# Folding a modulation row into expert rows, and re-ordering three starts, in a two-layer trunk kernel on Trainium2

## The chip, the cores and the metric

The kernel runs on one core of one Trainium2 chip. The metric is device microseconds (us) of one execution, and the time of a version is the median of its runs. The core has TensorE (PE) for matrix products, VectorE (DVE), ScalarE (ACT) and GpSimd (POOL) for the rest, and SyncE (SP), which here only issues transfers. PE's clock has two levels, 1.2 and 2.4 GHz; a granted clock of 0.50 in a row is the lower one and 1.00 the higher.

## The reference

Two layers run over 256 latent tokens and 256 context tokens of 1024 numbers. Each has a mixer part and an expert part, and each part ends in a residual sum whose second term is multiplied by a row of the modulation (`g1`, `g2`; `cg1`, `cg2` for context tokens). Layer 1 is the last one, and its context tokens are not computed beyond the keys.

```python
def rmsnorm(x, g):
    xf = x.astype(jnp.float32)
    y = xf * lax.rsqrt(jnp.mean(xf * xf, axis=-1, keepdims=True) + EPS)
    return (y * g.astype(jnp.float32)).astype(x.dtype)
...
    for e in range(N_EXPERTS):
        a = jax.nn.silu(t @ w_gate[e]) * (t @ w_up[e])
        y = y + gate[:, e:e + 1] * (a @ w_down[e])
...
        h = modulate(rmsnorm(x_lat, norm1_g[l]), sh1, sc1)
...
        x_lat = x_lat + g1 * hybrid_mixer(p, u, v, q_a, g, keys, lp, rope_tabs)
        h2 = modulate(rmsnorm(x_lat, norm2_g[l]), sh2, sc2)
        x_lat = x_lat + g2 * moe(h2, router_w, router_b, w_e_gate[l], w_e_up[l], w_e_down[l])
        if not last:
...
            x_ctx = x_ctx + cg2 * moe(hc2, router_w, router_b, w_e_gate[l], w_e_up[l], w_e_down[l])
```

`gate` is zero but for a token's two chosen experts, so only chosen pairs of token and expert are computed.

## The kernel before

Tokens lie in tiles of 128 partitions: t = 0 and 1 are latent, t = 2 and 3 context. Products that need full precision are done as three matmuls on high and low halves (`mm3`, L201 to L203): ACT casts the high half (L209 for weights), and `low` (L195) subtracts it to get the low half. `low` counts its calls in `spl[0]` and gives every fourth to GpSimd, the others to VectorE (`L198` is the subtraction of both). The order on each engine is the order of the code as a scheduler releases it, with `issue_after`, `behind` and `keep_in_program_order` as hand-set edges.

**Start (to 50 us).** The modulation is a product of the condition vector with a large weight that arrives in pieces. Each piece is four matmuls (L254); after the fourth of a group, ACT evicts the sum (L259), PE transposes it (L265) and DVE reduces it. `x_half(0)` and `x_half(1)` make the two halves of the normed, modulated input `xh` and `xl`; the second half needs the second group of pieces. `win_k` (L433) multiplies `xh` and `xl` with the weights of the columns `kr` and `kv0`.

**First dispatch (498 to 540 us).** After the router, `pick` (L1125) finds each token's two experts in a chain of small DVE operations, beside which `warm(5)` keeps PE busy with products that nobody reads. `first_idx` (L1152) ranks the tokens. Experts' work is cut into *jobs*: 128/g places of one expert, each row cut into g parts that lie in different partitions (g is 2 or 4). Job 0's tokens are picked by matmuls with a one-hot matrix (`dispatch`, L1171), which reads the rows in SBUF. Job 1's tokens are listed (`first_list`, L1189) and gathered from DRAM by GpSimd (`gather`, L1301). Then GpSimd scatters the lists of all places to DRAM in eight instructions (L1247), and gathers the tokens of jobs 2 and 3. Each job's rows are transposed on PE (L1419), copied by ACT (L1560) and multiplied with the gate and up weights (L1655); a SiLU on ACT (L1681), a product on DVE and a transposition (L1631) follow.

**Down (`down`, L1577).** The down product of a job (L1586) lies in PSUM as `py`. In layer 0 ACT scales it by the token's weight into `y2` (L1595), casts it to the high half and DVE makes the low half (L1603 to L1608), and PE adds both to the accumulators `acc` of the latent tokens with a one-hot matrix (L1620). `y2` is also scattered to DRAM for the context tokens. In layer 1 DVE does the scaling and multiplies with the modulation row `g2x` in one instruction (L1593). There are 25 downs in layer 0.

**Layer boundary (811 to 854 us).** `keep` (L1711) multiplies each quarter of `acc` with the row `g2b` (L1714), adds it to the residual `xres` (L1715) and takes its sum of squares on ACT (L1716). Two weights are split ahead (L1796), one low half on DVE and one on GpSimd. A loop for overflowing places (L1727) is tested and, in the profiled execution, not entered. `x_pair` (L364) takes the root from the sums, transposes and scales both latent tiles and makes `xh` and `xl`, on which PE starts the input products of layer 1. `comb` (L1802) reads the context tokens' expert rows back from DRAM as `yk`, adds the two of a token and multiplies them with a row on GpSimd (L1808, L1809), and adds them to `xres` on DVE (L1810). `x_tr` (L343) norms and transposes the two context tiles, and the `kr` product (L201 at 853.77 us) is the first that needs them.

Of the kernel before, what the change touches and what calls it, by code (L numbers as in the profile page):

```python
# [105 lines left out]
def trunk(ctx: ExitStack, tc: tile.TileContext, a, out):  # L106
# [195 lines left out]
    for l in range(DEPTH):  # L302
# [118 lines left out]
        if l == 0:  # L421
# [32 lines left out]
            win_k("kr", range(2, 4))  # L454
            win_k("kv0", range(4))
# [869 lines left out]
        pends = []  # L1325
# [182 lines left out]
        acc = [[atp() for _ in range(2)] for _ in range(2)]  # L1508
# [32 lines left out]
        if last:  # L1541
            place()
            for q_ in order_[7:9]:
                early[q_] = wexp(*q_, parts=4)
# [32 lines left out]
        def down(j, aT, wd):  # L1577
# [385 lines left out]
```

## Time and profile before

| quantity | value |
|---|---|
| median of 3 runs | 1314.17 us (1310.4 to 1314.49) |
| profiled execution | 1316.32 us, span 1314.7 us, mean granted clock 0.978 |
| PE busy | 1222.2 us, 93% of the span |
| DVE, ACT, POOL busy | 610.3, 406.9, 273.3 us |
| PE waits over 0.3 us, 480 to 840 us | 23.1 us in 17 waits; the longest 4.75, 3.99 and 3.40 |

The span runs from the first to the last recorded instruction. PE is busy nearly all the time, so a change shows in the whole time where it removes a wait of PE, moves work off PE, or lifts its clock. The rows of the trace give the wait ahead of an instruction in brackets, with the engine and the line that ended it.

### The profile page before, as it was taken

The page shows a single profiled execution, that of the slowest core. Times are in us where ns is not written, and L with a number is a line of the kernel's source. Part 1 is how long each engine was busy: PE and PEld are TensorE (multiplying, and loading weights), DVE is VectorE, ACT ScalarE, POOL GpSimd, SP SyncE. Part 2 cuts the span into 40 slices and gives each one's busy share as a digit, 9 for nine tenths or more (in the row PEclk, how much of TensorE's full clock was granted, in tenths as well). Part 3 has the DMA queues.
Part 4 walks back from the last instruction along what each step waited for, and adds up shares of the span by engine and source line. Part 5 has one row for each costly group of instructions (what it writes and reads, how often), then busy time and mean ns, then how long its engine had stood idle before and what let it go on. Part 6 is the DMA issues. An engine that isn't in the chain of part 4 may idle for free. (4 is left out here: it accounts for less than half of the span.)

```text
span 1314.7 us, 23115 instructions
## 1 busy us (share of the span) xinstructions
PE 1222.2 (93%) x9372; PEld 826.7 (63%) x9372; DVE 610.3 (46%) x1374; ACT 406.9 (31%) x765; POOL 273.3 (21%) x300
## 2 busy tenths in 40 slices
PE   5899989999999998899999998799999999888986
PEld 2587656666777775555555554678988965455544
DVE  4436554546332465332222324837666854534232
ACT  4433334333222221132122223544565421111112
POOL 0324350001201012221122111535610212100000
PEclk8899999999999998999999999899999999999999
DMA  8622465657655949498999835634444589999996
GB/s 343 200 60 73 145 226 213 222 193 235 209 180 191 314 156 354 178 412 333 397 402 423 332 140 209 229 121 134 127 157 142 189 331 356 423 424 421 423 425 251
DMA packets 70639, 338.30 MB, mean 257 GB/s; under 512 B 9472, under 2 KB 21168, under 8 KB 57984
## 3 DMA queue, kind: packets, MB, share of 16 engines
q1 hardware_dynamic: 59328, 320.93, 65.2%
q0 software_dynamic: 4832, 8.09, 1.8%
q10 hardware_dynamic: 6368, 7.76, 1.7%
q8 instruction: 75, 1.23, 0.4%
q14 instruction: 36, 0.29, 0.1%
HBM read 332.37 MB, written 10.02 MB: 260 GB/s over the span
## 5 line engine op out<-in xcount | busy, mean ns | idle before, releaser
L1655 PE MATMUL mmp<-wx,wh 128*64 128x256 f32 (+1 forms) x3456 | 254.8, 329 | 9.9 <-ACT wh L1560 6.1
L1655 PEld LDWEIGHTS mmp<-wx,wh 128*64 128x64 f32 (+1 forms) x3456 | 161.5, 124 | 94.4 <-issue 34.9
L201 PE MATMUL mmp<-xh,wh 128*128 128x512 f32 (+2 forms) x576 | 210.6, 367 | 6.8 <-ACT xh L430 6.1
L203 PE MATMUL mmp<-xh,wl 128*128 128x512 f32 (+2 forms) x576 | 201.4, 350 | 0.0
L1586 PE MATMUL trp<-wx,r 128*32 128x256 f32 (+1 forms) x944 | 130.1, 480 | 7.3 <-DVE r L1633 7.3
L201 PEld LDWEIGHTS mmp<-xh,wh 128*128 128x128 f32 (+1 forms) x576 | 109.9, 192 | 31.5 <-ACT xh L430 6.6
L203 PEld LDWEIGHTS mmp<-xh,wl 128*128 128x128 f32 (+1 forms) x576 | 110.4, 192 | 18.4 <-issue 2.9
L202 PE MATMUL mmp<-xres,wh 128*128 128x512 f32 (+1 forms) x288 | 115.5, 402 | 0.0
L209 ACT CAST wh<-raw 128x1024 fp32r<-128x1024 f32 (+2 forms) x53 | 54.0, 1024 | 127.6 <-PE mmp L202 51.6
L202 PE MATMUL mmp<-xl,wh 128*128 128x256 f32 (+2 forms) x288 | 86.8, 301 | 5.2 <-DVE xl L391 5.1
L1586 PEld LDWEIGHTS trp<-wx,r 128*32 128x32 f32 (+1 forms) x944 | 44.6, 122 | 73.2 <-issue 52.1
L198 DVE TENSOR_TENSOR wl<-raw,wh 128x1024 fp32r<-128x1024 f32 (+2 forms) x44 | 52.6, 1197 | 80.9 <-ACT wh L209 80.6
L1604 DVE TENSOR_TENSOR wl<-r,wl 64x512 fp32r<-64x512 f32 x54 | 37.1, 686 | 97.6 <-ACT wl L1603 85.7
L209 ACT CAST wh<-wx 128x1024 fp32r<-128x1024 f32 (+2 forms) x55 | 55.9, 1025 | 56.7 <-issue 24.1
L1425 POOL DMA_INDIRECT ysd<-r,ixh x25 | 25.5, 1022 | 192.8 <-ACT r L1595 192.2
L1595 ACT ACTIVATE r<-trp,sel 128x512 f32<-128x512 f32 (+1 forms) x25 | 15.5, 619 | 161.7 <-PE trp L1586 160.1
L202 PEld LDWEIGHTS mmp<-xres,wh 128*128 128x128 f32 (+1 forms) x288 | 54.6, 190 | 16.0 <-DVE xres L431 2.3
L1682 DVE TENSOR_TENSOR r<-r,mmp 128x256 f32<-128x256 f32 (+1 forms) x43 | 15.9, 370 | 103.5 <-ACT r L1681 103.5
L202 PEld LDWEIGHTS mmp<-xl,wh 128*128 128x128 f32 (+1 forms) x288 | 56.1, 195 | 11.3 <-DVE xl L391 5.8
L1620 PE MATMUL atp<-wl 128*128 128x512 f32 (+1 forms) x176 | 48.8, 416 | 12.3 <-ACT wl L1607 7.3
L198 DVE TENSOR_TENSOR wl<-wx,wh 128x1024 fp32r<-128x1024 f32 (+1 forms) x44 | 55.9, 1280 | 7.3 <-ACT wh L209 7.1
L1302 POOL DMA_INDIRECT wh<-h2d,ixh x24 | 27.6, 1149 | 127.7 <-PE trp L1419 94.8
(390 smaller groups left out, 2045.6 us busy)
## 6 DMA issues: line engine op xcount, KB each, us to landing
wx<-in_wexp_dram SPq DMA_DIRECT2D x79, 2048.0 KB
raw<-in_wmod_dram SPq DMA_DIRECT2D x80, 512.0 KB
wx<-in_wexp_dram SPq DMA_DIRECT2D x44, 512.0 KB
raw<-in_win_dram SPq DMA_DIRECT2D x35, 512.0 KB
wx<-in_win_dram SPq DMA_DIRECT2D x35, 512.0 KB
raws<-in_wmod_dram SPq DMA_DIRECT2D x8, 1024.0 KB
xres<-in_wexp_dram SPq DMA_DIRECT2D x5, 1024.0 KB
trk<-in_wexp_dram SPq DMA_DIRECT2D x5, 1024.0 KB
```

Source lines behind the costliest of these rows:

```text
L198: e.tensor_tensor(dst, full, hi.bitcast(F32), op=OP.subtract)
L201: T.matmul(o, lh, rh, start=first, stop=False, skip_group_check=True)
L202: T.matmul(o, lh, rl, start=False, stop=False, skip_group_check=True)
L203: T.matmul(o, ll, rh, start=False, stop=last_, skip_group_check=True)
L209: S.copy(h[:, :n], src)
L1302: return G.indirect_dma_start(out=xg[:, :D // g], out_offset=None, in_=h2d.rearrange("r (h d) -> (r h) d", h=g), in_offset=bass.IndirectOf ...
L1425: s_i = G.indirect_dma_start(out=ysd.rearrange("r (h d) -> (r h) d", h=g), in_=y, in_offset=None, out_offset=bass.IndirectOffsetOnAxis(ap= ...
L1586: T.matmul(py[i * P // g:(i + 1) * P // g, :w], aT[:, (c % m) * P + c // m * (P // g):(c % m) * P + (c // m + 1) * (P // g)], wcols(wd, o, ...
L1604: V.tensor_tensor(hb[1][rs, cs], y2[rs, :w], yh_.bitcast(F32), op=OP.subtract)
L1620: T.matmul(acc[t][h], one[h][rs, t * P:(t + 1) * P], hb[n][rs, h * 512:(h + 1) * 512], start=(j == 1 and n == 0 and not last), stop=(n == ...
L1655: parts(g, lambda h, gs_: mms.append(T.matmul(px[gs_, i * f:(i + 1) * f], ex[:, (k % n) * P + k // n * q:(k % n) * P + (k // n + 1) * q], ...
L1682: misc["a0"] = V.tensor_tensor(a0[:, :f], a0[:, :f], px[:, f:2 * f], op=OP.mult)
```

## The change

It has seven parts.

1. *Pieces first.* At the start, `kr`'s second half of products is put behind the first piece of the second modulation group, and `kv0`'s behind the second.
2. *Early accumulators.* `warm(5)` becomes `warm(1)` and four products of the identity with `xres`, which open `acc` with the residual in it.
3. *Both first places in SBUF.* Job 1's tokens are picked by `dispatch` too; `first_list(1)` and its gather go.
4. *Row folded.* In layer 0, `y2` is made as in layer 1, by DVE with the row `g2x`; ACT makes a second copy without the row, `yc`, for the scatter. Twelve small transfers bring `g2x`, and the transfer of `g2b` goes.
5. *Shorter `keep`.* It copies `acc` to `xres` on DVE, and ACT squares straight from `acc`. Both low halves ahead are on DVE, the second behind the sum of squares. The root is begun before the pools of the expert part close.
6. *Combine later.* The first addition of `yk` waits for `x_pair`'s last `xl`.
7. *No early low halves on GpSimd.* `spl[0]` is set to -8 in `x_pair`, so the next 15 calls of `low` go to DVE.

```diff
 def x_pair():
+            rs = misc["rs"]
+            spl[0] = -8
...
-            win_k("kr", range(2, 4))
-            win_k("kv0", range(4))
+            with tc.issue_after(misc["mod", 1, 0].ins):
+                win_k("kr", range(2, 4))
+            with tc.issue_after(misc["mod", 1, 1].ins):
+                win_k("kv0", range(4))
...
-            dispatch(0, one_hot(0, r2([P, NT, P // fixed[0][2]])), False)
+            hots = [one_hot(n, r2([P, NT, P // fixed[n][2]])) for n in range(2)]
...
-            first_list(1)
-            gather(xgb[1], fixed[1][2], ix01[:, 1:2])
+            for n in range(2):
+                dispatch(n, hots[n], False)
...
-                warm(5)
+                warm(5 if last else 1)
+                for t_ in range(2):
+                    for h in range(2):
+                        acc[t_][h] = atp()
+                        if not last:
+                            tc.keep_in_program_order(T.matmul(acc[t_][h], ident, xres[:, t_, h * 512:(h + 1) * 512],
+                                                              start=True, stop=False, skip_group_check=True))
...
-            if last:
-                V.scalar_tensor_tensor(y2[:, :w], py[:, :w], sel[:, k, 2:3], g2x[g, b], op0=OP.mult, op1=OP.mult)
-            else:
-                S.activation(y2[:, :w], py[:, :w], AF.Copy, scale=sel[:, k, 2:3])
+            V.scalar_tensor_tensor(y2[:, :w], py[:, :w], sel[:, k, 2:3], g2x[g, b], op0=OP.mult, op1=OP.mult)
...
+            if not last:
+                yc = r2([P, 512])
+                S.activation(yc[:, :w], py[:, :w], AF.Copy, scale=sel[:, k, 2:3])
+                scatter(yc[:, :w], g, ixh[:, k, 1:2])
             halves(evict)
-            if not last:
-                scatter(y2[:, :w], g, ixh[:, k, 1:2])
...
-            tm = r2([P, 512])
-            V.tensor_tensor(tm, v, g2b[:, hs], op=OP.mult)
-            V.tensor_tensor(xres[:, t, hs], xres[:, t, hs], tm, op=OP.add)
-            S.activation(tm, xres[:, t, hs], AF.Square, accum_out=misc["ss"][:, t, hf:hf + 1])
+            S.activation(tm, x_ if more else v, AF.Square, accum_out=misc["ss"][:, t, hf:hf + 1])
...
-            G.tensor_tensor(yk[:, 1], yk[:, 1], yk[:, 0], op=OP.add)
+            behind(G.tensor_tensor(yk[:, 1], yk[:, 1], yk[:, 0], op=OP.add), misc["xl", 1])
```

At the start, PE's second group of pieces before (L254 is a piece, L265 the transposes of the finished group, L201 to L203 the products):

```order
L203 MATMUL mmp<-xh,wl 128x512
L201 MATMUL mmp<-xh,wh 128x512
L254 MATMUL atp<-raws,trk 32x512 x4
L202 MATMUL mmp<-xres,wh 128x512
L203 MATMUL mmp<-xh,wl 128x512
L254 MATMUL atp<-raws,trk 32x512 x4
L265 MATMUL trp<-st_69,r_286 128x128 x4
```

And after, from the second and third piece on:

```order
L254 MATMUL atp<-raws,trk 32x512 x8
L201 MATMUL mmp<-xh,wh 32x512
L202 MATMUL mmp<-xres,wh 32x512
L203 MATMUL mmp<-xh,wl 32x512
L201 MATMUL mmp<-xh,wh 32x512
L202 MATMUL mmp<-xres,wh 32x512
L203 MATMUL mmp<-xh,wl 32x512
L254 MATMUL atp<-raws,trk 32x512 x4
L201 MATMUL mmp<-xh,wh 128x512
L202 MATMUL mmp<-xres,wh 128x512
L203 MATMUL mmp<-xh,wl 128x512
L201 MATMUL mmp<-xh,wh 128x512
```

Before, all 24 products of `kr` and `kv0` stand ahead of the group's last piece. After, 12 do; 4 more stand between that piece and the transposes, and 8 behind the transposes.

At the first dispatch, PE before (L1177 is the pick of job 0, L1198 the lists, L1419 the transposes of a job's rows):

```order
L1177 MATMUL trp<-xh,r_4154 64x512 x8
L1198 MATMUL trp<-cst,r_4168 128x1 x4
L1198 MATMUL trp<-cst,r_4274 128x1 x4
L1198 MATMUL trp<-cst,r_4282 128x1 x4
L1419 MATMUL trp<-st_69,wh 128x128 x4
L1655 MATMUL mmp<-wx_3689,wh 64x256 x16
L1655 MATMUL mmp<-wx_3691,wh 64x256 x8
L1419 MATMUL trp<-st_69,wh 128x128 x2
L1655 MATMUL mmp<-wx_3691,wh 64x256 x8
L1655 MATMUL mmp<-wx_3689,wh 32x128 x32
```

And after:

```order
L1176 MATMUL trp<-xh,r_4158 64x512 x8
L1176 MATMUL trp<-xh,r_4160 32x256 x16
L1197 MATMUL trp<-cst,r_4282 128x1 x4
L1197 MATMUL trp<-cst,r_4290 128x1 x4
L1424 MATMUL trp<-st_69,wh 128x128 x6
L1655 MATMUL mmp<-wx_3689,wh 64x256 x16
L1655 MATMUL mmp<-wx_3691,wh 64x256 x16
L1655 MATMUL mmp<-wx_3689,wh 32x128 x32
```

The two transposes of job 1 have moved from within job 0's products (64x256) to before them, and 16 picking products stand where one list did.

At the layer boundary, VectorE before, from the sum of squares on (L391 are the four `xl` of `x_pair`, L1810 the context tiles' sums):

```order
L366 TENSOR_TENSOR ss<-r_ssx 128x2
L160 TENSOR_SCALAR rs<-ss 128x2
L372 TENSOR_SCALAR r_7008<-st_69,rs 128x128 x2
L386 TENSOR_SCALAR r_7016<-trp,gsc,modcol_86 128x256
L386 TENSOR_SCALAR r_7026<-trp,gsc,modcol_86 128x256
L391 TENSOR_TENSOR xl<-r_7016,xh 128x2x256
L198 TENSOR_TENSOR wl<-wx_6993,wh 128x1024
```

And after (L1806 is the second low half ahead, L1820 the context tiles' sums):

```order
L1798 TENSOR_TENSOR ss<-r_ssx 128x2
L1806 TENSOR_TENSOR wl<-wx_6671,wh 128x1024
L160 TENSOR_SCALAR rs<-ss 128x2
L369 TENSOR_SCALAR r_7072<-st_69,rs 128x128 x2
L383 TENSOR_SCALAR r_7080<-trp,gsc,modcol_86 128x256
L198 TENSOR_TENSOR wl<-wx_7062,wh 128x1024
L388 TENSOR_TENSOR xl<-r_7080,xh 128x2x256
```

A low half of 1024 columns now stands between the sum of squares and the root, and another ahead of the first `xl`. Behind the last `xl`, the context sums have taken this order (L613 reads products of PE):

```order
L198 TENSOR_TENSOR wl<-wx_7062,wh 128x1024
L198 TENSOR_TENSOR qal<-r_7171,qah 128x256
L613 TENSOR_SCALAR r_7202<-mmp,trk 128x256
L1820 TENSOR_TENSOR xres<-xres,yk 128x1024
L198 TENSOR_TENSOR qal<-r_7202,qah 128x256
L613 TENSOR_SCALAR r_7238<-mmp,trk 128x256
L1820 TENSOR_TENSOR xres<-xres,yk 128x1024
```

The second context sum has two more operations between it and the first, where one L160 stood before.

## Rows read from the trace of the kernel before

**Rows 1.** Windows by stage: PE, PEld, DVE, ACT, POOL busy; clock, DMA share, GB/s.
```profile
570.00:640.00 70.00, 70.00 (x633) 39.00 (x633) 17.74 (x40) 17.74 (x34) 13.27 (x12) 1.00 0.91 368
854.00:1000.00 146.00, 143.33 (x1023) 124.91 (x1021) 86.40 (x179) 74.61 (x138) 57.31 (x70) 0.98 0.43 134
1090.00:1308.00 218.00, 192.78 (x2256) 112.50 (x2252) 87.66 (x214) 33.37 (x72) 17.05 (x17) 1.00 0.97 400
```

**Rows 2.** Timeline, PE, at the start: start, length, instruction, [idle before].
```profile
36.08 0.39 PE L203 MATMUL mmp<-xh,wl 128*128 128x512 f32 x1
36.31 0.39 PE L201 MATMUL mmp<-xh,wh 128*128 128x512 f32 x1
...
38.28 1.06 PE L254 MATMUL atp<-raws,trk 128*32 128x512 f32 x8
40.05 0.65 PE L265 MATMUL trp<-st,r 128*128 128x128 f32 x4 [0.71 <-ACT r L259]
44.09 1.06 PE L201 MATMUL mmp<-xh,wh 128*32 128x512 f32 x2 [3.38 <-ACT xh L430]
```

**Rows 3.** Windows at the start.
```profile
42.60:49.40 6.80, 5.31 (x13) 2.99 (x14) 4.54 (x9) 3.98 (x8) 1.94 (x6) 0.50 1.02 392
49.40:60.00 10.60, 10.60 (x49) 8.07 (x47) 7.33 (x9) 6.16 (x9) 7.57 (x15) 1.00 0.61 170
```

**Rows 4.** Timeline, PE, at the first dispatch.
```profile
516.63 7.09 PE L1655 MATMUL mmp<-wx,wh 128*64 128x256 f32 x48 [0.67 <-ACT wh L1560]
523.65 0.44 PE L1419 MATMUL trp<-st,wh 128*128 128x128 f32 x2
...
530.72 3.77 PE L1655 MATMUL mmp<-wx,wh 128*32 128x128 f32 x66 [4.75 <-ACT wh L1560]
...
534.79 1.07 PE L1655 MATMUL mmp<-wx,wh 128*32 128x128 f32 x30
```

**Rows 5.** Timeline, ACT, at the first dispatch.
```profile
530.29 0.37 ACT L1560 COPY wh<-trp 128x256 f32<-128x256 f32 x1 [13.71 <-remote]
```

**Rows 6.** Timeline, POOL, at the first dispatch.
```profile
515.89 1.03 POOL L1247 DMA_INDIRECT lst<-tokid,r_ai  x1 [0.30 <-DVE r_ix L1200]
...
526.14 1.04 POOL L1302 DMA_INDIRECT xg<-h2d,r_ix  x1 [0.30 <-issue]
```

**Rows 7.** Line L1593 (layer 1): length in ns (min, median, max), first and last.
```profile
L1593 DVE SCALAR_TENSOR_TENSOR r<-trp,sel,wh x10: 750/751/752, 1109.4 to 1276.1; 128x512 f32<-128x512 f32 x10
```

**Rows 8.** Timeline, DVE, at the layer boundary.
```profile
814.70 2.60 DVE L1715 TENSOR_TENSOR xres<-xres,r 128x512 f32<-128x512 f32 x2
...
817.83 1.21 DVE L1796 TENSOR_TENSOR wl<-wx,wh 128x1024 fp32r<-128x1024 f32 x1
818.96 0.68 DVE L1715 TENSOR_TENSOR xres<-xres,r 128x512 f32<-128x512 f32 x1
...
825.67 0.69 DVE L391 TENSOR_TENSOR xl<-r,xh 128x512 fp32r<-128x512 f32 x1
826.49 3.20 DVE L198 TENSOR_TENSOR wl<-wx,wh 128x1024 fp32r<-128x1024 f32 x1
829.62 2.83 DVE L391 TENSOR_TENSOR xl<-r,xh 128x512 fp32r<-128x512 f32 x1
...
833.58 4.42 DVE L391 TENSOR_TENSOR xl<-r,xh 128x512 fp32r<-128x512 f32 x2 [0.23 <-ACT xh L390]
...
842.14 1.22 DVE L1810 TENSOR_TENSOR xres<-xres,yk 128x1024 f32<-128x1024 f32 x1
```

**Rows 9.** Timeline, POOL, at the layer boundary.
```profile
826.01 2.60 POOL L1808 TENSOR_TENSOR yk<-yk 128x1024 f32<-128x1024 f32 x1 [4.10 <-DMA yk<-ysd]
...
834.75 2.70 POOL L1809 TENSOR_TENSOR yk<-yk,g2c 128x1024 f32<-128x1024 f32 x1
```

**Rows 10.** Timeline, PE, at the layer boundary.
```profile
822.38 2.02 PE L379 MATMUL trp<-r,xres 128*128 128x128 f32 x16 [3.40 <-DVE r L372]
...
853.77 0.65 PE L201 MATMUL mmp<-xh,wh 128*32 128x512 f32 x2 [0.70 <-ACT xh L361]
```

More of the change, by code (lines that the diff above doesn't have):

```diff
@@ L1323, in decide @@
                     order()
-        pends = []
+        pends, acc = [], [[None] * 2 for _ in range(2)]
         for hf in range(2):
@@ L1507, in trunk @@
         SPR, late_x = (1, -1) if last else (3, 3)
-        acc = [[atp() for _ in range(2)] for _ in range(2)]
         ixh = mo.tile([P, NCOL[l], 2], I32, name="ixh")
@@ L1553, in trunk @@
                 early[q_] = wexp(*q_, nc.sync, parts=4)
+        for (g, b), v in g2x.items():
+            for i in range(g):
+                q = 3 * KD + (i + b * g // 2) % g * KD // g
+                nc.sync.dma_start(v[i * P // g:(i + 1) * P // g].rearrange("p (k q) -> p k q", q=P),
+                                  modrow[l].rearrange("(k r) q -> r k q", r=2)[0:1, q:q + KD // g, :].to_broadcast(
+                                      [P // g, KD // g, P]))
         ws, adds = {0: w0}, []
@@ L1620, in add @@
                             T.matmul(acc[t][h], one[h][rs, t * P:(t + 1) * P], hb[n][rs, h * 512:(h + 1) * 512],
-                                     start=(j == 1 and n == 0 and not last), stop=(n == 1 and j == len(jobs) - 1), skip_group_check=True)
+                                     start=False, stop=(n == 1 and j == len(jobs) - 1), skip_group_check=True)
             if b or j == len(jobs) - 1:
@@ L1785, in trunk @@
                         if not last:
-                            keep(t, g, pz)
+                            keep(t, g, pz, True)
                     if last:
@@ L1793, in trunk @@
             break
-        for e, v in zip((V, G), pre_split.values()):
+        ss = st.tile([P, 2, 1], F32, name="ss")
+        s_ = V.tensor_tensor(ss, misc["ss"][:, :, 0:1], misc["ss"][:, :, 1:2], op=OP.add)
+        misc["rs"] = st.tile([P, 2], F32, name="rs")
+        misc["pow", 1] = rstd(misc["rs"], ss.rearrange("p t o -> p (t o)"), 1.0 / D)
+        for n, v in enumerate(pre_split.values()):
             lo = wk.tile([P, 1024], F32R, name="wl", bufs=3)
-            e.tensor_tensor(lo, v[1], v[0].bitcast(F32), op=OP.subtract)
+            with ExitStack() as es_:
+                if n:
+                    es_.enter_context(tc.issue_after(s_.ins))
+                V.tensor_tensor(lo, v[1], v[0].bitcast(F32), op=OP.subtract)
             v[1] = lo
```

37 lines of the change are left out of this document (14 added, 23 removed).

## The prediction

> **What bounds the kernel now.** I read the windows by stage first [rows 1]. From 570 to 640 us PE is busy in 70.00 of 70.00 us at clock 1.00, so in layer 0's experts only PE's own work counts. From 854 to 1000 us it is 143.33 of 146.00. From 1090 to 1308 us the DMA share is 0.97, so layer 1's experts follow their weights; those transfers are issued as buffers come free, so an earlier start moves them too. What is left to win are PE's waits at three places: the start, the first dispatch and the layer boundary. I read those in the timelines, engine beside engine. A difference within 0.3% (4 us) I call no change.
>
> **The start.** The last piece runs at 38.28, the transposes wait 0.71 us for ACT and start at 40.05, and 4.04 us later, after a wait of 3.38 us, the second half's products start at 44.09 [rows 2]. After the change 12 products fewer stand ahead of the last piece. Two neighbours start 0.23 us apart (36.08, 36.31), so the piece ends 12 x 0.23 = 2.8 us earlier. Then four products (0.92 us) stand ahead of the transposes, in place of the 0.71 us wait, so the transposes come 0.2 us less early: 2.55 us. The chain from there to the second half is unchanged and the other eight products (1.85 us) fill part of its wait, at no cost. So 2.5 us. From 42.6 to 49.4 the clock is 0.50, behind these waits [rows 3]; with 1.5 us of wait left there are 5.3 us of work, which at full clock would take 2.6 less. Whether the shorter wait keeps the clock is open: I take 1.0 of it, in all **3.5** (0 if the pieces' data are not there so early, since no row shows their landing; 5.1 with the clock). From 49.4 on PE is busy in 10.60 of 10.60 us [rows 3], so the gain is kept.
>
> **Early accumulators.** Four products of the same shape take the place of four fillers in a chain that PE waits for anyway: 0.
>
> **The first dispatch.** Job 0's products start at 516.63, job 1's transposes are recorded at 523.65, and job 1's products start at 530.72 after a wait of 4.75 us [rows 4]. The wait is ended by ACT's copy of those transposes, which starts only at 530.29, after 13.71 us of idling that the view puts to "remote" [rows 5]. So the copy came 6 us behind the end of the transposes that it reads, and no row explains that. After the change the transposes stand ahead of job 0's products, and their copy has 9 us of cover. The pieces of the sum:
> - The wait goes: 4.75.
> - 66 matmuls took 3.77 us behind it, and 30 later ones of the same shape 1.07 [rows 4], so at that pace 66 take 2.4: 1.4 for the clock.
> - Job 0 itself: the 16 new picking products have twice the columns of those 30 and, at two records each, cost 16 x 2 x 0.07 = 2.2 us, but the one list that goes frees PE and an operation of DVE; an estimate of 0.6 gained.
>
> What is late next? Job 2's rows. Their gather is issued at 526.14 behind eight scatters that started at 515.89 [rows 6]. With job 1's gather gone the scatters start some 2 us earlier, so the gather does too; PE reaches job 2's transposes at about 528.5 in place of 535, so it is a close call. Job 2's weights stand behind four of the twelve new transfers. Sum 6.7; for the unexplained delay I take **5.5**. The low end is 1.7: the same delay strikes job 2 or the weights.
>
> **The fold.** In each of 25 downs DVE gets one more instruction, 0.75 us for 512 columns [rows 7], at most 25 x 0.75 = 18.8 us. It takes the place of ACT's scaling on the path to the halves, and ACT's own copy runs beside it. PE, busy without a wait from 570 on [rows 1], hides it; uncovered are only the first downs and the last ones, where PE waits for the halves: **-0.5** (0 to -1.5). The twelve transfers hide behind weights that are needed tens of us later, but for job 2's above.
>
> **The layer boundary.** Before, `keep`'s last addition ended at 818.96 + 0.68 = 819.64 [rows 8], and `x_pair` started on PE at 822.38 [rows 10], 2.74 us later; between them lay ACT's last square (0.7 by the addition of the same tile), the loop's test, the sum and the root. Two additions began at 814.70 [rows 8], each behind a product of its own, so `acc` is complete by 814.70 - 2 x 0.69 = 813.3. After: the last two copies (1.4) and a low half (1.21 by its twin at 817.83) end at 815.9; the 2.74 lose the square, which runs beside the low half, and gain the second low half (1.21): 3.25. So `x_pair` starts at about 819.2. In `x_pair` DVE's low half took 3.20 beside `yk`, against 1.21, and the `xl` 2.83 and 4.42 for two against 0.69 each [rows 8]: 2.0 + 2.1 + 3.0 = 7.1 us of stretch. Moving `yk` behind the last `xl` takes that away: the last `xl` was done at 833.58 + 4.42 = 838.0, 15.6 us after the start, and is now done 8.5 us after it, at 827.7. Then `yk` runs; its four instructions took 11.4 us (826.01 to 834.75 + 2.70 [rows 9]), so to 839.1. Before, they ended at 837.45: the combination gets *later* though `x_pair` is earlier. Who waits for it are the two context sums, the second of which started at 842.14 and led to `kr` 11.6 us later, at 853.77 [rows 8, 10]. Between these ends:
> - The second sum can start as `yk` ends, 839.1: `kr` at 850.7, 3.1 gained.
> - The first sum meets GpSimd's fourth instruction, as the low half at 826.49 met the first one: that began at 826.01, took 2.60, and the low half ended 1.08 us behind its end [rows 8, 9]. Then the first sum ends at 840.2, two operations on 256 columns follow (0.9 by estimate, from 0.69 for 512), and the second sum starts at 841.1: `kr` at 852.7, 1.1 gained.
>
> The Trainium skill's page "SBUF — State Buffer", section "Who interferes with whom", says that a VectorE instruction with two SBUF inputs contends with a GpSimd instruction that reads SBUF, and that the one that comes second is blocked for the whole of the other. By that rule, the trace agrees with 1.08 us behind, the second of the two ends is right, and the sum below would be some 0.7 us less.
>
> I take 1.8 between them, and 0.8 back for the clock, as PE will have nothing to do from about 840 on: **+1.0**, with -3 (the whole chain from `yk`'s end as long as before, 853.77 - 837.45 = 16.3 us, and the clock) and +4 as ends.
>
> **Low halves on DVE.** The next 15 calls of `low` cost DVE up to 1.21 each [rows 8] and free GpSimd of a part of them. DVE is busy in 86.4 of 146 us there and PE waits 2.7 us in all [rows 1], so 0 (1.5 either way).
>
> **The sum.** 3.5 + 5.5 - 0.5 + 1.0 + 0 = 9.5. The profiled execution took 1316.32 us, so 1306.8; it lies 2.15 over the median of the runs shown, so **1304.7**.
>
> **The rivals.**
> - *The delay at 530 stays.* Against it: the copy has 9 us of cover. For it: nothing explains the delay, so nothing says that the transposes' place matters. PE would work through job 1 and then stall at the next thing it needs: 1.7 in place of 5.5, 1308.5. Chance 0.15.
> - *The combination bounds the boundary.* `yk` ends 2 us later than before, and if the context tiles' chain is as long as it was, `kr` starts later than before: -3 in place of +1, 1308.7. For it: the two additions now come ahead of both multiplications, so the first tile too has to wait for three instructions. Chance 0.13. With the one above, 1312.5: 0.09.
> - *The blocking rule decides.* The second end above and more of such meetings among the moved low halves: `kr` at 852.7, 0.7 less, and some 1.5 of the low halves' range: about 1306.9. For it: the stretched rows; against it: GpSimd has less to do after the boundary. Chance 0.10.
> - *Slower: the fold reaches PE.* A down's halves wait for the added DVE instruction, ahead of it the SiLU product and the copies of other jobs queue on DVE, and PE's additions wait in every job. All of it uncovered costs 18.8, so 1304.7 + 18.3 = 1323; it decides from about half of it, 9.5 us, or 0.4 us a down. Against it: not one wait of PE in 70 us. Chance 0.11.
> - *My forecast:* 0.42, with 1300 to 1309 as its own range.
>
> **How the numbers follow.** Faster by over 0.3% is below 1310.2. The forecast (0.42) and the rule (0.10) lie there whole; the delay and the combination alone lie 1.5 us below that bound, so about two thirds of them, 0.18. Faster 0.70. The rest of these two, 0.10, and both together, 0.09: same 0.19. Slower 0.11. The best ends together (5.1 + 6.7 + 0 + 4 + 1.5 = 17.3) give 1296.9, so the range begins at 1297; to 1314 it takes in both failures together and leaves out the fold.
>
> **What would show it.** Right: second half's products at about 41.5 us; no wait of PE over 1 us between 516 and 540, and job 2's products some 6 us earlier, relative to the start of job 0; no new wait of PE from 570 to 800; `x_pair` some 3 us earlier behind the last addition, its `xl` at 0.69 each; `yk` later; a new wait of PE between 836 and 851, on the context tiles. Wrong: a wait of several us on job 2's gather or weights; PE waiting for `y2` or the halves in each job; `kr` no earlier than before, counted from the boundary; the clock low from 836 on for long.

## The result, and the profile after

The changed kernel took 1324.24 us (median of 6 runs, 1321.71 to 1329.29), the kernel before 1312.39 (6 runs, 1308.39 to 1314.49): a ratio of 1.0088, 95% interval 1.0068 to 1.0108. It is 11.6 us slower, where 9.5 us less were forecast. Below, a ratio is turned into microseconds as (ratio − 1) x 1314. The profiled execution took 1329.29 us, its span is 1327.7.

To see where the time went I compare the start of the same PE instruction in two traces. Each number is the median of (kernel minus before) over the instructions within 5 us of that time in the trace of before:

| kernel, parts | 366 us | 568 | 796 | 860 | 1000 | 1070 | 1100 | 1180 | 1200 to the end |
|---|---|---|---|---|---|---|---|---|---|
| the change, 1 to 7 | −5.5 | −10.8 | −9.6 | −3.1 | +1.9 | +8.1 | +9.8 | +11.1 | +12.4 |
| e2, 1 to 5 and 7 | −5.3 | −10.3 | −9.1 | −8.7 | −3.9 | +2.1 | +3.7 | +5.0 | +6.3 |
| e1, 1 to 6 | −7.2 | −12.9 | −11.8 | −4.9 | −5.2 | −4.1 | −2.4 | −2.7 | −0.1 |
| e3, 1 to 5 | −5.8 | −11.3 | −10.2 | −9.9 | −10.2 | −9.0 | −7.3 | −7.4 | −7.8 |
| e14, 1, 2, 4, 5 | −7.3 | −8.5 | −7.3 | −9.2 | −9.5 | −8.8 | −7.1 | −7.2 | −4.6 |
| e12, 1 | −5.0 | −8.3 | −8.2 | −8.4 | −8.4 | −6.8 | −6.8 | −7.1 | −6.1 |
| e10, none (the kernel before) | −1.8 | +0.4 | +0.3 | +0.8 | +0.8 | +0.8 | +0.8 | +0.8 | +3.5 |

The first line tells the story: to 568 us all goes as forecast or better, layer 0's experts take 1.2 back, and then 22 us are lost, 6.5 at the boundary (796 to 860), 11.2 from 860 to 1070, and 4.3 behind that. The other kernels are explained below.

At the start and at the first dispatch the steps show as the prediction named them: the second half's products start at 40.41 in place of 44.09 [rows 2], and between 513.98 and 525.92 no wait is left where 4.75 us stood [rows 4]. Timeline of PE after (start, length, instruction, [idle before]):

```profile
40.41 0.64 PE L201 MATMUL mmp<-xh,wh 128*32 128x512 f32 x2 [0.93 <-ACT xh L427]
...
513.98 10.63 PE L1655 MATMUL mmp<-wx,wh 128*64 128x256 f32 x130 [0.46 <-ACT wh L1561]
...
525.92 0.66 PE L1424 MATMUL trp<-st,xg 128*128 128x128 f32 x4
```

The windows by stage after (columns as in [rows 1]) show that layer 0's experts are as full as before, and where PE now stands and runs at a lower clock; the first row is the start, where the clock was 0.50 before [rows 3]:

```profile
42.60:49.40 6.80, 6.80 (x33) 4.87 (x32) 4.58 (x7) 4.99 (x8) 5.61 (x13) 1.00 0.85 282
570.00:640.00 70.00, 69.84 (x604) 38.39 (x605) 21.13 (x43) 16.60 (x32) 13.50 (x12) 1.00 0.91 371
833.00:846.00 13.00, 7.68 (x41) 6.63 (x41) 11.78 (x17) 10.63 (x22) 4.10 (x4) 0.68 0.48 159
846.00:851.00 5.00, 3.58 (x14) 2.86 (x14) 3.96 (x8) 2.10 (x3) 1.27 (x1) 0.50 0.32 115
854.00:1000.00 146.00, 139.59 (x999) 123.45 (x997) 85.46 (x175) 71.37 (x132) 54.61 (x68) 0.97 0.39 120
```

From 854 to 1000 PE is busy in 139.59 us where it was 143.33 [rows 1]. Now the layer boundary after, PE first:

```profile
805.12 6.33 PE L1308 MATMUL mmp<-cst,st 128*128 128x512 f32 x8
812.10 2.02 PE L376 MATMUL trp<-r,xres 128*128 128x128 f32 x16 [0.64 <-DVE r L369]
...
839.65 1.07 PE L350 MATMUL trp<-st,xn 128*128 128x128 f32 x8 [1.80 <-DVE xn L340]
842.59 1.98 PE L350 MATMUL trp<-st,xn 128*128 128x128 f32 x8 [1.87 <-ACT r L358]
...
851.41 0.64 PE L202 MATMUL mmp<-xl,wh 128*32 128x512 f32 x1 [1.83 <-DVE xl L362]
...
903.59 0.79 PE L202 MATMUL atp<-wl,kvh 128*128 128x512 f32 x1 [4.12 <-DVE wl L198]
```

DVE beside it:

```profile
811.66 0.48 DVE L369 TENSOR_SCALAR r<-st,rs 128x128 f32<-128x128 f32 x2 [2.09 <-PEq L1730]
...
816.32 1.23 DVE L198 TENSOR_TENSOR wl<-wx,wh 128x1024 fp32r<-128x1024 f32 x1 [1.85 <-ACT wh L209]
...
821.98 0.55 DVE L383 TENSOR_SCALAR r<-trp,gsc,modcol 128x256 f32<-128x256 f32 x1 [1.41 <-ACT r L385]
823.21 0.69 DVE L388 TENSOR_TENSOR xl<-r,xh 128x512 fp32r<-128x512 f32 x1 [0.69 <-ACT xh L387]
...
827.05 2.83 DVE L198 TENSOR_TENSOR wl<-wx,wh 128x1024 fp32r<-128x1024 f32 x1 [0.48 <-ACT wh L209]
...
832.70 3.00 DVE L1820 TENSOR_TENSOR xres<-xres,yk 128x1024 f32<-128x1024 f32 x1
...
836.35 1.21 DVE L1820 TENSOR_TENSOR xres<-xres,yk 128x1024 f32<-128x1024 f32 x1
...
839.42 1.22 DVE L198 TENSOR_TENSOR wl<-wx,wh 128x1024 fp32r<-128x1024 f32 x1
...
843.50 1.23 DVE L198 TENSOR_TENSOR wl<-wx,wh 128x1024 fp32r<-128x1024 f32 x1
...
848.80 1.96 DVE L198 TENSOR_TENSOR wl<-wx,wh 128x1024 fp32r<-128x1024 f32 x1
```

And GpSimd:

```profile
824.04 4.76 POOL L1818 TENSOR_TENSOR yk<-yk 128x1024 f32<-128x1024 f32 x2 [13.66 <-DVE xl L388]
828.75 5.86 POOL L1819 TENSOR_TENSOR yk<-yk,g2c 128x1024 f32<-128x1024 f32 x2
```

- `x_pair` starts at 812.10 in place of 822.38 [rows 10], 10.3 us earlier, against 9.6 at the end of layer 0's experts: 0.7 gained where some 3 were worked out. DVE had its sum and root ready, but waited 2.09 us for the loop's test on PE's queue (PEq L1730), and that stands behind PE's own four fillers (L1308, eight records, 6.33 us).
- The four `xl` are no longer stretched (0.69 us for the last), as forecast. But the last one ends at 823.90, 11.8 us after the start of `x_pair`, where 8.5 had been worked out: between them DVE now waits for ACT, 1.85 and 1.41 us, at places that showed no wait before.
- The combination runs from 824.04 to 834.61 (826.01 to 837.45 before [rows 9]). Its first sum on DVE ends at 835.70, 1.09 us behind GpSimd's last instruction; the second starts at 836.35, against 842.14 [rows 8], so 5.8 us of the 10.3 are still ahead here.
- From the second sum to the `xl` that PE waits for at 851.41 lie three low halves of 1024 columns on DVE (839.42, 843.50, 848.80). From the start of the second sum to this product (L202, the first of `kr` that reads `xl`) it was 12.4 us before; after, it is 15.1. From the end of the combination to it, it was 17.1 and is 16.8, so this chain has stayed as long as it was. PE's clock is 0.68 from 833 to 846 and 0.50 to 851.

### The profile page after: what moved, and what is told of

The parts are those of the page before. It is cut to its first block, busy times and chain, and to the rows that moved or that the text cites. A ratio compares the mean times of both kernels' runs of the same rounds, so it can differ in the third digit from the quotient of the medians.

```text
span 1327.7 us, 23189 instructions
## 1 busy us (share of the span) xinstructions
PE 1232.0 (93%) x9396; PEld 832.3 (63%) x9396; DVE 626.8 (47%) x1396; ACT 404.3 (30%) x766; POOL 270.1 (20%) x297
## 5 line engine op out<-in xcount | busy, mean ns | idle before, releaser
L201 PE MATMUL mmp<-xh,wh 128*128 128x512 f32 (+2 forms) x576 | 210.4, 367 | 7.6 <-ACT xh L427 3.6
L203 PE MATMUL mmp<-xh,wl 128*128 128x512 f32 (+2 forms) x576 | 200.6, 349 | 0.0
L201 PEld LDWEIGHTS mmp<-xh,wh 128*128 128x128 f32 (+1 forms) x576 | 110.0, 191 | 34.3 <-issue 5.1
L203 PEld LDWEIGHTS mmp<-xh,wl 128*128 128x128 f32 (+1 forms) x576 | 110.0, 191 | 16.1 <-DVE wl L198 1.0
L202 PE MATMUL mmp<-xres,wh 128*128 128x512 f32 (+1 forms) x288 | 114.6, 398 | 0.1
L209 ACT CAST wh<-raw 128x1024 fp32r<-128x1024 f32 (+2 forms) x53 | 54.0, 1024 | 125.7 <-PE mmp L202 49.2
L198 DVE TENSOR_TENSOR wl<-raw,wh 128x1024 fp32r<-128x1024 f32 (+2 forms) x44 | 52.7, 1199 | 79.8 <-ACT wh L209 79.5
L202 PE MATMUL mmp<-xl,wh 128*128 128x256 f32 (+2 forms) x288 | 86.3, 300 | 2.7 <-DVE xl L362 1.8
L209 ACT CAST wh<-wx 128x1024 fp32r<-128x1024 f32 (+2 forms) x55 | 56.1, 1025 | 71.6 <-PE mmp L202 37.7
L1593 DVE SCALAR_TENSOR_TENSOR r<-trp,sel,wh 128x512 f32<-128x512 f32 x27 | 20.3, 751 | 109.8 <-PE trp L1587 109.8
L198 DVE TENSOR_TENSOR wl<-wx,wh 128x1024 fp32r<-128x1024 f32 (+2 forms) x45 | 61.6, 1371 | 20.2 <-ACT wh L209 19.8
L202 PEld LDWEIGHTS mmp<-xres,wh 128*128 128x128 f32 (+1 forms) x288 | 54.2, 188 | 14.7 <-DVE r L426 1.7
L1430 POOL DMA_INDIRECT ysd<-r,ixh x25 | 26.7, 1070 | 175.1 <-ACT r L1611 173.9
L202 PEld LDWEIGHTS mmp<-xl,wh 128*128 128x128 f32 (+1 forms) x288 | 56.1, 195 | 8.7 <-issue 3.4
L1620 PE MATMUL atp<-wl 128*128 128x512 f32 (+1 forms) x176 | 49.4, 421 | 12.3 <-ACT wl L1605 8.0
```

What stands on the lines that cost most here:

```text
L198: e.tensor_tensor(dst, full, hi.bitcast(F32), op=OP.subtract)
L201: T.matmul(o, lh, rh, start=first, stop=False, skip_group_check=True)
L202: T.matmul(o, lh, rl, start=False, stop=False, skip_group_check=True)
L203: T.matmul(o, ll, rh, start=False, stop=last_, skip_group_check=True)
L209: S.copy(h[:, :n], src)
L1430: s_i = G.indirect_dma_start(out=ysd.rearrange("r (h d) -> (r h) d", h=g), in_=y, in_offset=None, out_offset=bass.IndirectOffsetOnAxis(ap= ...
```

## The experiments

They are told apart by the seven parts of the change. Four groups, e1 to e4, e5 to e8, e9 to e11 and e12 to e15, each ran on one chip, beside the kernel before on that chip. e10 is one more execution of the kernel before and has no ratio.

| run | parts | ratio to before | 95% | us |
|---|---|---|---|---|
| the change | 1 to 7 | 1.0088 | 1.0068 to 1.0108 | +11.6 |
| e1 | 1 to 6 | 1.0003 | 0.9982 to 1.0024 | +0.4 |
| e2 | 1 to 5, 7 | 1.0050 | 1.0033 to 1.0066 | +6.6 |
| e3 | 1 to 5 | 0.9950 | 0.9933 to 0.9967 | −6.6 |
| e4 | 1, 3 | 0.9952 | 0.9930 to 0.9974 | −6.3 |
| e5 | 1 to 5, 7 with −10 | 0.9984 | 0.9960 to 1.0008 | −2.1 |
| e6 | 1 to 5, 7 with 92 | 1.0038 | 1.0017 to 1.0059 | +5.0 |
| e7 | 2, 4, 5 | 1.0022 | 0.9998 to 1.0045 | +2.9 |
| e8 | 1 | 0.9943 | 0.9924 to 0.9962 | −7.5 |
| e9 | 3 | 1.0028 | 1.0002 to 1.0054 | +3.7 |
| e11 | 1 to 5, half the fillers | 0.9957 | 0.9938 to 0.9977 | −5.7 |
| e12 | 1 | 0.9945 | 0.9928 to 0.9961 | −7.2 |
| e13 | 1, 3 | 0.9964 | 0.9944 to 0.9983 | −4.7 |
| e14 | 1, 2, 4, 5 | 0.9986 | 0.9969 to 1.0004 | −1.8 |
| e15 | 1 to 5 | 0.9973 | 0.9958 to 0.9988 | −3.5 |

### Which parts lose it: e1 to e4

The theory from the trace was that parts 6 and 7 lose everything behind 812 us; the rival, that part of the early gain never reaches the end.

```diff
 e1, against the changed kernel
-            spl[0] = -8
 e2, against the changed kernel
-            behind(G.tensor_tensor(yk[:, 1], yk[:, 1], yk[:, 0], op=OP.add), misc["xl", 1])
+            G.tensor_tensor(yk[:, 1], yk[:, 1], yk[:, 0], op=OP.add)
 e3: both; e4: the kernel before with parts 1 and 3
```

> The changed kernel, with the line that sets the counter of low halves to -8 taken out; GpSimd takes every fourth low half again, as before the change. Theory A (the moved low halves cost most): in the changed kernel's trace the distance to the kernel before goes from -3.7 us at 896 us to +9.8 at 1090; it should stay near -3 here, so the time falls by 10 to 13 us against the changed kernel (1324), to 1311 to 1314. Theory B (the later combination of the context tiles is what costs): the time falls by 0 to 3 us.

> The changed kernel, with the first addition of the context rows no longer behind the last xl. Theory B (the later combination costs): the first product that needs the context tiles lost 7.2 us against the start of x_pair; these come back, and the time falls by 5 to 7 us from 1324, to 1317 to 1319. Theory A (low halves): what is gained at the boundary is lost again at the low halves near 903 us, where PE already waits for DVE; the time falls by under 2 us.

> The changed kernel without both: low halves shared as before, combination not behind. If both cost, and add up, some 17 us come back: 1305 to 1308, below the kernel before by 0.4 to 0.6%. If the two are one cost seen twice, the same as the better of the two others, 1311 to 1314.

> The kernel before, with only the pieces first and both first places picked in SBUF. In the changed kernel's trace the two gained 5.5 and 5.6 us by 555 us. Theory 1 (the gain is real and passes on, since PE and the transfers behind it follow): 1312.4 - 11 = 1301 to 1303. Theory 2 (the gain is swallowed behind, by the transfers of layer 1's weights): 1309 to 1312.

Parts 6 and 7 cost 18 us together (e3 against the change), so they turn the sign. Part 7 costs 13.2 us alone (e2 against e3) and 11.2 beside part 6; part 6 costs 7.0 alone (e1 against e3) and 5.0 beside part 7. But e3 and e4 stop at 6.5 us gained, not at the 10 to 11 that they have at 796 us (e3 −10.2, e4 −11.1): the rival holds too. What e3 and e4 lose behind 1000 us goes in steps of 1 to 2 us between 1050 and 1190; that the transfers of the weights swallow it, as theory 2 has it, is not shown. By the medians e2 (1322.5) came out as its theory A said and e4 (1309.0) as its theory 2; e1 (1316.0) lies between its two theories, e3 (1309.3) 1.3 above what was expected.

One caution on sizes: e15 is the same kernel as e3 on another chip and gained 3.5 us, not 6.6. Measured from e15, each cost above and below that is counted from e3 alone is 3.0 us smaller (15 for both parts, 10.1 for part 7, 3.9 for part 6); the signs stay.

How part 6 loses can be read in e1 and e3. DVE in e1, where the combination comes behind the last `xl`:

```profile
824.87 2.77 DVE L198 TENSOR_TENSOR wl<-wx,wh 128x1024 fp32r<-128x1024 f32 x1 [0.48 <-ACT wh L209]
827.57 2.58 DVE L198 TENSOR_TENSOR qal<-r,qah 128x256 fp32r<-128x256 f32 x1
830.46 4.68 DVE L1819 TENSOR_TENSOR xres<-xres,yk 128x1024 f32<-128x1024 f32 x2
```

DVE in e3, where it need not:

```profile
826.93 3.42 DVE L1819 TENSOR_TENSOR xres<-xres,yk 128x1024 f32<-128x1024 f32 x1
...
830.68 1.21 DVE L1819 TENSOR_TENSOR xres<-xres,yk 128x1024 f32<-128x1024 f32 x1
```

Windows at the boundary, of e1:

```profile
833.00:850.00 17.00, 10.10 (x43) 8.45 (x43) 11.43 (x23) 12.42 (x23) 6.33 (x6) 0.50 0.39 124
```

And of e3:

```profile
833.00:850.00 17.00, 13.61 (x83) 9.76 (x82) 11.02 (x22) 11.70 (x23) 6.52 (x6) 0.90 0.56 186
```

In e1 the low half and the `qal` that lead to PE's next products are stretched to 2.77 and 2.58 us beside GpSimd's additions, and both context sums end together at 835.1; in e3 they end at 830.3 and 831.9, while PE still has `x_pair`'s products. PE's matmul behind that (`kr`, L201), in e3 and then in e1:

```profile
844.14 1.04 PE L201 MATMUL mmp<-xh,wh 128*32 128x512 f32 x2 [0.70 <-ACT xh L361]
```

```profile
847.41 1.04 PE L201 MATMUL mmp<-xh,wh 128*32 128x512 f32 x2
```

It starts 3.3 us later in e1, though e1 was 1.6 us ahead of e3 before the boundary: 4.9 us, and PE's clock is 0.50 in this stretch of e1, 0.90 in e3. In the table part 6 takes 6.9 us in e1 and 6.5 in the change between 796 and 860, and 0.3 (e3) and 0.4 (e2) are lost there without it.

### What in part 7 costs: e5 and e6

Followed through the calls, `spl[0]` stands at 90 when `x_pair` begins (the trace has 90 instructions of L198 ahead of it). −8 does two things: the next 15 calls go to DVE, and, since every fourth call is GpSimd's, the turn of all later calls moves by two (90 leaves 2 when divided by 4, −8 leaves 0). So two kernels part them, both without part 6: −10 keeps the early low halves on DVE and the old turn, 92 moves the turn alone.

```diff
 e5, against e2
-            spl[0] = -8
+            spl[0] = -10
 e6, against e2
-            spl[0] = -8
+            spl[0] = 92
```

> As e2 (combination not behind), but the counter is set to -10 in place of -8. The first low halves of layer 1 still all go to DVE, and from the fifth that GpSimd takes on they are the same calls as in e3, since -10 and the old count of 90 leave the same rest modulo 4. Theory A1 (the shift of the count by two is what costs: GpSimd gets the low halves of two other weights and of xl at 1036 to 1066 us, and another one near 893 us): about e3, 1309 to 1312. Theory A2 (the early low halves on DVE cost): about e2, 1319 to 1323. Both in halves: the 4 us wait near 893 us stays and the waits from 1035 us on go, about 1315.

> As e2, but the counter is set to 92: GpSimd keeps its early low halves, every fourth call from the fourth on, and the calls are those of the changed kernel later on (same rest modulo 4 as -8). Theory A1 (the shift): about e2, 1319 to 1323, with waits on DVE low halves at 1035 to 1050 us. Theory A2 (the early ones on DVE): about e3, 1309 to 1312.

The early low halves on DVE cost 4.5 us (e5 against e3; 1.4 against e15), the turn 11.6 alone (e6 against e3; 8.5 against e15) and 8.7 in e2 against e5, which differ by nothing else. e6 came out as the theory of the turn said, e5 (1313.0) between that theory (to 1312) and half of each (1315). By the instruction, e5 loses 2.4 us to e3 between 835 and 850, where DVE runs early low halves ahead of the context tiles' `xn`, and 1.5 more at about 1180. e2 is level with e5 from 825 to 848, about 1 ahead of it to 893, 4.0 behind at 899, 5.3 at 1033 and 9.2 from 1055 on. PE, DVE and GpSimd of e2:

```profile
897.99 0.80 PE L202 MATMUL atp<-wl,kvh 128*128 128x512 f32 x1 [4.14 <-DVE wl L198]
```

```profile
896.72 1.22 DVE L198 TENSOR_TENSOR wl<-wx,wh 128x1024 fp32r<-128x1024 f32 x1
...
1035.68 1.94 DVE L971 TENSOR_TENSOR r<-r,r 128x256 f32<-128x256 f32 x1
...
1040.23 3.29 DVE L198 TENSOR_TENSOR wl<-wx,wh 128x1024 fp32r<-128x1024 f32 x1
```

```profile
890.95 2.40 POOL L198 TENSOR_TENSOR wl<-wx,wh 128x1024 fp32r<-128x1024 f32 x1
...
1034.78 2.56 POOL L198 TENSOR_TENSOR wl<-wx,wh 128x1024 fp32r<-128x1024 f32 x1
...
1040.05 2.40 POOL L198 TENSOR_TENSOR xl<-wx,xl 128x1024 fp32r<-128x1024 f32 x1 [0.36 <-ACT xl L209]
```

And of e5:

```profile
895.35 0.50 PE L202 MATMUL atp<-wl,kvh 128*128 128x512 f32 x1 [0.58 <-DVE wl L198]
```

```profile
894.08 1.22 DVE L198 TENSOR_TENSOR wl<-wx,wh 128x1024 fp32r<-128x1024 f32 x1
```

```profile
1046.24 2.36 POOL L198 TENSOR_TENSOR wl<-wx,wh 128x1024 fp32r<-128x1024 f32 x1 [8.51 <-ACT wh L209]
```

The waits of PE from 1025 to 1070 us (in total, times, longest), two of e2 and one of e5:

```profile
PE atp L201 <- DVE r L968: 1.9, 3, 0.8
PE atp L202 <- DVE wl L198: 1.3, 1, 1.3
```

```profile
PE atp L201 <- DVE r L968: 0.6, 2, 0.3
```

In e5 two low halves stand early in DVE's chain of the pool mixer, and the second, which PE needs, ends at 895.30. In e2 the first is GpSimd's (890.95) and the second stands behind the whole chain, so PE waits 4.14 us. Later, in e2, two low halves of GpSimd fall among DVE's last ones of the mixer's output; DVE's instructions beside them take 1.94 in place of 0.41 and 3.29 in place of 1.21, and they feed PE, which waits for them 3.2 us in place of 0.6. In e5 GpSimd's one low half comes at 1046.24, when DVE has no such work. The changed kernel has the turn of e2, and the same wait at 903.59.

### The first dispatch: e7 to e10, and the table e12 to e15

```diff
 e8 (part 1), against the kernel before
-            win_k("kr", range(2, 4))
-            win_k("kv0", range(4))
+            with tc.issue_after(misc["mod", 1, 0].ins):
+                win_k("kr", range(2, 4))
+            with tc.issue_after(misc["mod", 1, 1].ins):
+                win_k("kv0", range(4))
 e9 (part 3), against the kernel before
-            dispatch(0, one_hot(0, r2([P, NT, P // fixed[0][2]])), False)
+            hots = [one_hot(n, r2([P, NT, P // fixed[n][2]])) for n in range(2)]
...
-            first_list(1)
-            gather(xgb[1], fixed[1][2], ix01[:, 1:2])
+            for n in range(2):
+                dispatch(n, hots[n], False)
 e7: parts 2, 4 and 5 of the change alone; e10: the kernel before once more
 e12 as e8; e13 as e4; e14: parts 1, 2, 4 and 5; e15 as e3
```

> The kernel before with the folded row, the early accumulators, the shorter keep and the second low half ahead on DVE; start, first dispatch, combination and low halves as before. From the trace of the changed kernel: 1.5 to 2 us lost in layer 0's experts, 1 to 2 gained up to x_pair; 0 to -1.5 against before. If the fold reaches PE in each down: slower by 5 us or more.

> The kernel before with the pieces first alone. The start gained 5.5 us in the changed kernel's trace; 3 to 5.5 us faster than before if it passes on. The first dispatch is as before here, so this also shows whether the wait of 4.75 us behind job 0 is there again: if it is a fixed property of that order, 4 to 5 us of waiting at about 525 us; if it was a chance event of one execution, none.

> The kernel before with both first places picked in SBUF alone. e4 (start and dispatch) and e8 (start alone) have the same median, 1309.0 and 1308.4, though e8's profiled execution lost 7.8 us to a gather. Theory F (the wait on a gather behind job 0 is in nearly every execution before): 4 to 6 us faster than before. Theory C (a gather is late in some executions only): faster by 0 to 2 us in the median, with no wait of over 2 us behind job 0 in the profile.

> The kernel before once more, for a second trace of the same program. Theory F: a wait of 4 to 8 us behind job 0 again. Theory C: another length, or none. In layer 1's experts the first trace had clock 1.00 throughout; if the drop near 1185 us in other traces belongs to their programs, it's 1.00 again; if it is chance, it may fall here too.

> Part 1 alone, once more, as the base of a table of four on one chip: with and without part 3, with and without parts 2, 4 and 5. The trace of the start's change says 5.5 to 7.4 us saved, so a ratio to before of 0.994 to 0.996.

> Parts 1 and 3. Theory A (the wait at the first dispatch goes, but 16 more picking products and the clock take its place): the same as part 1 alone, within 2 us. Theory B (the trace's gain of about 4 us is kept to the end): 4 us less than part 1 alone, a ratio of 0.991 to 0.993.

> Parts 1, 2, 4 and 5: the prediction's start, accumulators, fold and shorter boundary, without the new dispatch, the later combination and the count. If the parts simply add, part 1's ratio plus the 0.0022 that parts 2, 4 and 5 cost alone: 0.9965. If the shorter boundary is kept here, 1 to 3 us less than part 1 alone: 0.992 to 0.994.

> Parts 1 to 5. It differs from the run with parts 1, 2, 4 and 5 by part 3 alone. Theory A: the same as that within 2 us. Theory B: 4 us less. Earlier it stood at 0.995.

The new dispatch brings nothing in the time: +3.7 us alone (e9), +1.2 and +2.5 beside part 1 (e4 against e8; e13 against e12, one chip), −1.7 beside parts 1, 2, 4 and 5 (e15 against e14, one chip). The four average to a loss of 1.4, with intervals of some 3 us each; for e9 both theories, which had it faster, missed. In the traces it does gain: from 366 to 568 us the change, e1, e2, e3, e4, e13 and e15 win 5.0 to 5.7 us; but e9 wins 0.6 there and e11 loses 0.5. With the old dispatch the same stretch lies between 3.5 lost and 3.3 won (e8, e10, e7, e14, e12), so against the trace beside it on its chip the new one wins 2.8 (e9 against e10), 2.3 (e13 against e12) and 4.5 us (e15 against e14). The price, in PE's timeline of e9:

```profile
509.50 6.83 PE L1177 MATMUL trp<-xh,r 128*64 128x512 f32 x48 [0.64 <-PE trp L1210]
...
520.99 12.15 PE L1655 MATMUL mmp<-wx,wh 128*64 128x256 f32 x130 [0.49 <-issue]
```

And in e10:

```profile
507.49 5.47 PE L1177 MATMUL trp<-xh,r 128*64 128x512 f32 x16 [0.64 <-PE trp L1210]
...
517.32 7.09 PE L1655 MATMUL mmp<-wx,wh 128*64 128x256 f32 x48 [0.68 <-ACT wh L1560]
...
531.25 3.68 PE L1655 MATMUL mmp<-wx,wh 128*32 128x128 f32 x66 [4.60 <-ACT wh L1560]
```

From the pick to job 0's first product it is 11.49 us in e9 and 9.83 in e10: 1.7 us for the 16 more picking products and what follows. The wait that goes is 4.60 us here, and it was 4.75 in the first trace of the same program [rows 4]. With the edits beside it, the old dispatch waits at other places and for other things: one row each of PE in e7, e8, e12 and e14, in this order:

```profile
521.34 0.66 PE L1421 MATMUL trp<-st,wh 128*128 128x128 f32 x2 [5.23 <-DMA wh<-h2d,r_ix]
```

```profile
530.34 1.08 PE L1421 MATMUL trp<-st,xg 128*128 128x128 f32 x4 [7.78 <-DMA xg<-h2d,r_ix]
```

```profile
528.79 0.63 PE L1421 MATMUL trp<-st,xg 128*128 128x128 f32 x4 [2.34 <-DMA xg<-h2d,r_ix]
```

```profile
514.35 0.66 PE L1423 MATMUL trp<-st,wh 128*128 128x128 f32 x2 [4.43 <-DMA wh<-h2d,r_ix]
```

Here the view names a gather from DRAM that GpSimd has issued, of job 1's rows (`wh`) or of job 2's (`xg`). e8 and e12 are one program, and it waited 7.78 us in one execution and 2.34 in another; the 7.78 belong to e8's longest execution (1315.06; its median is 1308.37). So each of the six traces of the old dispatch has a wait of 2 to 8 us, but not the same one. The "remote" of the kernel before [rows 5] is something else by what is on record: of job 1's gather its trace holds 6 of 16 landings, at 520.20 to 520.65, and e10's 6, at 520.70 to 520.83, ahead of the transposes that read the rows (523.65 and 524.34), while the copy starts at 530.29 and 530.83. Why the copy is late stays unexplained, as it was in the prediction; that it is so in both traces of that program speaks against chance.

Without parts 6 and 7, profiled executions with the old dispatch lie above their kernel's median by 2.2 (before), 6.7 (e8) and 3.7 (e12), or near it (−0.3 for e14, 0.6 for e7, 0.7 for e10), those with the new one by 1.3 at most (e4, e13, e15, e3, e9): the traces of before, e8 and e12 are of executions longer than usual. That accounts for a part of the gap between trace and time; where the rest goes is open.

The start alone (e8, e12) has the largest gain: 7.5 and 7.2 us, faster than both kernels, though the intervals of e3 and e4 reach as far. Parts 2, 4 and 5 cost 5.4 us beside it (e14 against e12), 1.2 in the other half of the table (e15 against e13), and 2.9 alone (e7); e7 and e14 came out slower than expected. Of this the fold is 1.1 to 1.2 us, by the table of places from 568 to 796 (the change, e1 to e3, e14); the shorter boundary gives 1.9 in e14 and nothing in e3. The rest goes between 1000 and 1200 us, where all kernels with the old turn lose 1 to 6, in steps of 1 to 3 us. Only the last step is shown to come without an edit: e10, the kernel before, loses 2.7 between 1180 and 1200. From 1000 to 1180 neither of its two traces loses anything, and every other kernel does. The last step in rows: the same 32 matmuls behind the same wait of 1.73 us, in the trace of before and in that of e10:

```profile
1183.96 3.67 PE L1655 MATMUL mmp<-wx,wh 128*64 128x256 f32 x32 [1.73 <-DVE wh L1567]
```

```profile
1184.77 6.46 PE L1655 MATMUL mmp<-wx,wh 128*64 128x256 f32 x32 [1.73 <-DVE wh L1567]
```

The granted clock from 1180 to 1200 is 1.00 in the first and 0.83 in the second. The program is the same, so the lower clock there is no effect of an edit; the trace that I predicted from happens to be one that kept full clock. What decides it was not found.

### The fillers at the boundary: e11

```diff
 e11, against e3
-            warm(4)
+            warm(2)
```

> e3 with two of the four fillers at the layer boundary. In e3's trace DVE waits 2.24 us for PE to leave the loop's test, behind the fillers, before x_pair starts. If that wait is what bounds x_pair: about 1 us earlier, since the root is ready 1.0 us before PE, and 1308 to 1309 against 1309.3. If the fillers' end is not the bound, no change; if fewer fillers cost the clock, slower by 1 to 2 us.

With two fillers in place of four the ratio is 0.9957, against 0.9950 and 0.9973 for e3 and e15: no gain that the time shows. In its trace 3.0 us are won from 796 to 860, where e3 loses 0.3, so up to 3 us may lie there, within the intervals.

## Why the prediction was wrong, point by point

- **The step that failed: "low halves on DVE, 0 (1.5 either way)".** It measured −13.2 (−11.2 beside part 6; −10.1 from e15). I counted DVE's work against its idle time, an average over 146 us, and counted the next 15 calls alone. The new number also moved the turn of every later call, and 8.7 to 11.6 us come from that (9.2 by the instruction, e2 against e5): two places, 903 and 1041 to 1061 in the changed kernel, where the low half or the DVE work beside it ends PE's wait. The rest, 1.4 to 4.5 us, is put to the early low halves; the trace shows 2.4 of it, where they stand on DVE in front of the context tiles' chain.
- **"The layer boundary, +1.0, −3 as low end".** It failed too: between 796 and 860 us the change lost 6.5, and part 6 alone measured −7.0. The rival "the combination bounds the boundary" had the right mechanism: `yk` ends later and the chain behind it is as long as before (16.8 us against 17.1), which by the prediction's own numbers is a `kr` 1.6 later (839.1 + 16.3, against 853.77). Two terms were mis-sized on top. Of 3.2 us worked out for `x_pair`'s start 0.7 came, since its wait moved to the loop's test behind PE's fillers: 2.5 more. And `yk` ended 22.5 us after that start in place of 19.9, since the last `xl` came after 11.8 in place of 8.5: 2.6 more. Together 6.7, against 6.5 measured. The clock was at 0.50 in a part of the stretch, and low halves stretched beside GpSimd stand ahead of PE's next products (e1).
- **The blocking rival.** Its rows came as told: the first sum ended 1.09 us behind GpSimd's fourth instruction. It was one part of the loss, not a case of its own.
- **"First dispatch, 5.5".** The wait went and no other took its place, as forecast; the time did not follow (−1.4, −3.7 to +1.7). The wait was no chance of one execution: the kernel before had it twice, 4.75 and 4.60. One term had the wrong sign: the 16 picking products cost 1.7 from pick to job 0, where I had a gain of 0.6. In the traces 2.3 to 4.5 us are left at 568 against a neighbour on the same chip, and why the time keeps none of it stays open. The rival that the delay stays, which gave 1.7, is nearer to the measured time, but its mechanism (a stall at the next thing that PE needs) did not happen.
- **"Start, 3.5".** The mechanism was right and both terms too small: the second half's products came 3.7 us earlier, where 2.5 were worked out, and 5.8 us were gained by 50 us, the other 2 at a clock of 1.00 from 42.6 to 49.4 where it was 0.50 [rows 3] and I took 1.0. Over all kernels with part 1 the traces have 4.6 to 9.5 at 366 us, those without it 0.5 to 2.8; the time has 7.2 and 7.5.
- **"Fold, −0.5".** Nearly right: 1.2 us, PE's busy time 69.84 in 70.00 us. The slower rival that I gave 0.11 (the fold reaches PE) named almost the measured time, 1323, by a mechanism that did not happen.
- **The sum.** In gains: start 7.3, dispatch −1.4, parts 2, 4 and 5 −1 to −5, parts 6 and 7 −18.1 (−15.1 from e15), in all −10 to −17 against −11.6 measured. The parts don't add exactly; parts 1 to 5 alone measured 6.6 and 3.5 gained on two chips.

## What to carry to other kernels

A counter that deals out work in turn is a schedule: resetting it moves every later piece of work, so list where each of them lands and what runs beside it, before the reset is costed at nothing. A shared engine's idle time over a long window says nothing of the place where it ends the bound engine's wait; look for the places where the trace names that engine as the releaser. A wait that ends with a gather from DRAM can differ threefold between two executions of one program (7.78 and 2.34 us here): take it from several before it is booked as a gain. And a wait that is gone from the trace is not yet time won: here it went in every trace, and the time did not follow.

## What the runs showed of the hardware

- DVE beside GpSimd: in the changed kernel a low half of 1024 columns that started at 827.05 ended at 829.88, 1.08 us behind GpSimd's second instruction (828.80), and the sum of 832.70 ended at 835.70, 1.09 behind the fourth (834.61). Alone such an instruction takes 1.21 us. So nearly the whole of it came behind GpSimd's. The Trainium skill's page "SBUF — State Buffer", section "Who interferes with whom", says that the one that comes second is blocked for the whole of the other; the trace agrees, with 1.08 and 1.09.
- TensorE's clock: the same program at the same place, behind the same wait, ran 32 matmuls in 3.67 us in one execution and in 6.46 in another (granted clock from 1180 to 1200 us 1.00 and 0.83). A lower clock in one trace is no property of the program until a second shows it.
- PE's wait for a gather of job 2's rows was 7.78 and 2.34 us in two executions of one program on two chips (e8, e12); for job 1's rows it was 5.23 and 4.43 in two programs with another order (e7, e14).
